# The down-projection of a gated MLP as seven products of half blocks in place of eight, with the sums of its left operands made in the up-projection's loop

## The chip, the cores and the metric

The kernel runs on one core of a Trainium2 chip. The metric is the device time of one execution in microseconds (us); the time quoted is the median of the runs shown. The engines are TensorE (PE, with its loads of the stationary operand as PEld), VectorE (DVE), ScalarE (ACT), GpSimd (POOL) and SyncE (SP), which in this kernel issues all DMA transfers.

## The reference

One encoder layer is applied to two sequences of 512 tokens with 1024 features, with shared weights. Only its last part, the gated MLP, is touched:

```python
h2 = _rmsnorm(x, g_ffn) * (1 + sc2) + sh2
u = _dwconv(h2 @ w_up, conv_w, conv_b)        # width 3, along the tokens
ua, ug = jnp.split(u, 2, axis=-1)             # 2816 features each
x = x + gt2 * ((jax.nn.silu(ug) * ua) @ w_down)
```

All arrays are float32, and the result is compared with a float32 reference, so a product of two matrices is made of three matmuls.

## The kernel before

**Split operands.** Each operand of a matmul is split into a high part (the value rounded to TensorE's fp32r format) and a low part (the rest). `mm3` (L78) multiplies high x high, high x low and low x high into one bank of PSUM. A split is a cast and a subtraction: `split_fast` (L74) makes the cast on ScalarE and the subtraction on VectorE, `split_pool` (L68) both on GpSimd.

**Order.** The code is written in program order, with tiles taken from pools of a fixed number of buffers. A scheduler that knows the dependencies and has a cost for each instruction puts the instructions of each engine into an order when the kernel is built; on the chip each engine, and SyncE's queue, goes through its list in that order.

**Up-projection** (L893 to L1007). It runs over 22 feature blocks `c` of 128 value and 128 gate features. Per block both sequences are made at once, as seven products of half blocks (12 matmuls each, `product`, L929) into three banks `px`, `py`, `pz`. The weights' sums for them are made on GpSimd (L913 to L919), the casts of the seven weight tiles on ScalarE, their subtractions on VectorE (four) and GpSimd (three) (`split_w`, L897). The products are copied and added into two value and two gate blocks; `conv1` (L941) makes the convolution in scratch tiles `tmp_u` of two buffers each; `gated` (L951) applies the gate, multiplies in place in the scratch tile and stores the product to the DRAM tensor `g_d`. Blocks 0 to 3 are started early, beside the last preparation of the activations.

**Down-projection** (L1009 to L1053). The two sequences follow each other. For a sequence all eight banks are taken, one for each of four token tiles and two halves of the 1024 output features. A loop over the 22 blocks of the contraction loads the activation block from `g_d` and the two halves of a weight block, splits them (activation and first half with `split_fast`, second half with `split_pool`) into a slot `wd` of four kinds (`pt`, `h`, `st`, `h`), and multiplies 24 matmuls. The last three blocks (`LATE`, L1014) are multiplied bank by bank, so that a bank is read out while the next ones are still multiplied. Reading out is a multiplication by the gate `gt` (L1051), an addition of the residual `xe` (L1052) and a store (L1053).

Raw weights and activations pass through six `wraw` tiles (L718), split weights of the up-projection through eight `wt` tiles (L723). The large tiles `h` (four buffers), `st` and `pt` (two each) hold the activations' halves of the up-projection: `st` holds `e` and then `t4`, `pt` holds `h1` and `h2`, `h` holds `e2`, `t3`, `t2` and `t1`.

## Time and profile before

| what | value |
|---|---|
| time, median of 3 runs (1461.2 to 1464.67) | 1461.97 us |
| span of the profiled execution, which was taken apart from these runs | 1468.5 us |
| down-projection, first to last matmul in that execution | 1222.97 to 1463.68 us |
| TensorE, VectorE, ScalarE, GpSimd busy | 96%, 68%, 46%, 41% |
| mean granted clock of TensorE, share of full speed | 0.985 |

Times in the rows below are from the span's start. Busy time of TensorE counts overlapping matmuls once, while the mean duration of one matmul contains the overlap with its neighbours. A row with `[x <- y]` says how long the engine stood idle before, and what ended that.

### The profile page before, as it was taken

What the parts mean: (1) busy time and instruction counts of PE and PEld (TensorE: products, weight loads), DVE (VectorE), ACT (ScalarE), POOL (GpSimd) and SP (SyncE); (2) the same over time, 40 slices, a digit from 0 to 9 for tenths busy, and PEclk for the clock granted to TensorE, in tenths of its full rate; (3) what the DMA queues carried; (4) which work ended last, traced back from release to release, by engine and by line L of the source; (5) the groups of instructions that cost most, each with busy time, mean ns of one, the idle gap of its engine ahead of it and who ended that gap; (6) DMA issues with size and microseconds to landing.
All of it is one profiled execution on the core that took longest, in us unless ns stands there. A gap on an engine that the chain in (4) does not pass through costs nothing.

```text
span 1468.5 us, 20794 instructions
## 1 busy us (share of the span) xinstructions
PE 1403.9 (96%) x7184; PEld 1161.6 (79%) x7184; DVE 1002.9 (68%) x1903; ACT 675.9 (46%) x1381; POOL 596.5 (41%) x600
## 2 busy tenths in 40 slices
PE   5889997999999999999998999999999999999998
PEld 4677876888888888878887777888888887888887
DVE  4788875666678886544479988777777777446433
ACT  3375222666666665422246455555555554122210
POOL 3365123442433442381004755555555535444430
PEclk9899999999999999999998999999999999999999
DMA  8456773222222213756302322222222227546522
GB/s 320 155 193 203 239 255 133 90 97 94 94 72 87 94 53 124 247 176 207 121 38 73 122 72 87 86 80 86 87 87 81 85 88 247 198 139 226 184 87 72
DMA packets 107801, 193.82 MB, mean 132 GB/s; under 512 B 18856, under 2 KB 39592, under 8 KB 104624
## 3 DMA queue, kind: packets, MB, share of 16 engines
q1 hardware_dynamic: 107696, 192.49, 39.6%
q8 instruction: 57, 0.93, 0.3%
q14 instruction: 48, 0.39, 0.1%
HBM read 148.39 MB, written 44.06 MB: 131 GB/s over the span
## 4 chain that ended last, share of the span: by engine, by line
PE 76%; DVE 15%; ACT 3%; POOL 2%; issue 2%; DMA 2%; SPq 0%; ACTq 0%; DVEq 0%; POOLq 0%
PE px L933 13%; PE psg L484 10%; PE py L933 6%; PE psd L81 5%; PE psd L79 5%; PE psd L80 5%; PE pz L933 3%; PE ppt L505 3%; PE ppo L568 2%; PE psz L79 2%; PE psx L81 2%; PE psx L80 2%; PE psx L79 2%; PE psz L81 2%; PE psy L81 2%
## 5 line engine op out<-in xcount | busy, mean ns | idle before, releaser
L933 PE MATMUL px<-t,wt 128*128 128x512 f32 x792 | 194.2, 395 | 7.6 <-ACT tmp_cc L938 6.6
L900 POOL TENSOR_TENSOR wt<-wraw,wt 128x512 fp32r<-128x512 f32 x66 | 91.5, 1390 | 238.3 <-ACT wt L899 238.2
L933 PEld LDWEIGHTS px<-t,wt 128*128 128x128 f32 x792 | 150.3, 191 | 42.1 <-ACT tmp_cc L938 9.4
L484 PE MATMUL psg<-h_hi,wg 128*128 128x512 f32 x512 | 169.8, 397 | 0.0
L499 POOL TENSOR_SCALAR p<-p,l 128x512 f32<-128x512 f32 (+2 forms) x128 | 78.2, 613 | 203.5 <-DVE l L498 128.8
L76 DVE TENSOR_TENSOR wd<-wraw,wd 128x512 fp32r<-128x512 f32 x88 | 95.5, 1124 | 94.5 <-ACT wd L75 94.4
L79 PE MATMUL psd<-wd 128*128 128x512 f32 x352 | 137.1, 389 | 1.3 <-DVE tmp_u L947 1.3
L81 PE MATMUL psd<-wd 128*128 128x512 f32 x352 | 137.0, 389 | 0.0
L80 PE MATMUL psd<-wd 128*128 128x512 f32 x352 | 136.9, 389 | 0.0
L75 ACT CAST wd<-wraw 128x512 fp32r<-128x512 f32 x88 | 50.9, 619 | 156.9 <-issue 108.4
L484 PEld LDWEIGHTS psg<-h_hi,wg 128*128 128x128 f32 x512 | 95.7, 189 | 18.4 <-POOL wg L72 0.8
L484 PE MATMUL psg<-h_lo,wg 128*128 128x512 f32 x256 | 101.6, 397 | 0.0
L497 ACT ACTIVATE p<-pps,nm 128x512 f32<-128x512 f32 (+2 forms) x128 | 78.1, 610 | 39.8 <-DVE nm L494 32.1
L945 DVE SCALAR_TENSOR_TENSOR tmp_u<-tmp_cc,cw,tmp_u 128x511 f32<-128x511 f32 x66 | 65.5, 993 | 39.4 <-ACT tmp_u L944 39.4
L900 DVE TENSOR_TENSOR wt<-tmp_sf,wt 128x512 fp32r<-128x512 f32 x88 | 82.2, 943 | 11.8 <-ACT wt L899 11.4
L79 PEld LDWEIGHTS psd<-wd 128*128 128x128 f32 x352 | 66.1, 188 | 15.5 <-issue 1.7
L69 POOL TENSOR_SCALAR wd<-wraw 128x512 fp32r<-128x512 f32 x44 | 30.6, 695 | 116.1 <-PE psd L81 77.9
L80 PEld LDWEIGHTS psd<-wd 128*128 128x128 f32 x352 | 66.1, 188 | 13.8
L494 DVE TENSOR_REDUCE nm<-pps 128x1 f32<-128x512 f32 (+2 forms) x128 | 74.7, 583 | 3.1 <-PE pps L81 1.5
L81 PEld LDWEIGHTS psd<-wd 128*128 128x128 f32 x352 | 66.1, 188 | 13.6
L72 POOL TENSOR_TENSOR wd<-wraw,wd 128x512 fp32r<-128x512 f32 x44 | 73.2, 1663 | 3.7
L947 DVE SCALAR_TENSOR_TENSOR tmp_u<-tmp_cc,cw,tmp_u 128x511 f32<-128x511 f32 x66 | 72.9, 1105 | 1.4
(257 smaller groups left out, 3516.0 us busy)
## 6 DMA issues: line engine op xcount, KB each, us to landing
w_ada<-in_w_ada_dram SPq DMA_DIRECT2D x24, 1024.0 KB, 6.3
wraw<-in_w_up_dram SPq DMA_DIRECT2D x96, 256.0 KB, 2.7
wraw<-in_w_down_dram SPq DMA_DIRECT2D x88, 256.0 KB, 3.5
g_d<-tmp_u SPq DMA_DIRECT2D x44, 256.0 KB, 2.3
wraw<-g_d SPq DMA_DIRECT2D x44, 256.0 KB, 3.4
wg_raw<-in_w_g_dram SPq DMA_DIRECT2D x16, 512.0 KB, 3.8
gate_d<-go SPq DMA_DIRECT2D x32, 256.0 KB, 2.0
ldb<-qb_d SPq DMA_DIRECT2D x8, 1024.0 KB, 5.0
```

The costliest lines, as they stand in the source:

```text
L72: G.tensor_sub(lo, raw, hi.bitcast(F32))
L76: V.tensor_sub(lo, raw, hi.bitcast(F32))
L79: PE.matmul(ps, lhsT=lh, rhs=rh, start=first, stop=False)
L80: PE.matmul(ps, lhsT=lh, rhs=rl, start=False, stop=False)
L81: PE.matmul(ps, lhsT=ll, rhs=rh, start=False, stop=last)
L484: PE.matmul(ps, lhsT=w[:, wl, m, k, :], rhs=hl[b][:, k, :], start=k == 0 and n == 0, stop=k == KD - 1 and n == 2)
L494: V.tensor_reduce(nm, ps[:, :n], op=ALU.max, axis=AX.X, negate=True)
L497: A.activation(p[:, :n], ps[:, :n], AF.Exp, bias=nm, accum_out=l)
L499: G.tensor_scalar(out=p[:, :plen], in0=p[:, :plen], scalar1=l, scalar2=1.0, op0=ALU.mult, op1=ALU.mult)
L900: lo_eng.tensor_sub(w[:, 1], raw, w[:, 0].bitcast(F32))
L933: PE.matmul(ps[:, sl], lhsT=w[:, wl, i], rhs=h[:, hl, sl], start=not add and i == 0 and n == 0, stop=i == 3 and n == 2, skip_group_check=add)
L947: V.scalar_tensor_tensor(out=u[:, 0:S - 1], in0=src[:, 1:S], scalar=cw[:, cc, 2:3], in1=u[:, 0:S - 1], op0=ALU.mult, op1=ALU.add)
```

## The change

The product of the activations A (rows: sequence 1, sequence 2; columns: blocks 0 to 10, blocks 11 to 21) and the weights B (the same halves of the contraction by two halves of the output features) is made as seven products of half blocks. Their left operands are A11, A12, A22, S1 = A21 + A22, S2 = S1 - A11, S3 = A11 - A21 and S4 = A12 - S2; their right operands are B11, B21, B22, and sums of blocks of B, kept in tiles `T`. Each product has 11 steps of 12 matmuls into a set of four banks; there are two sets.

In the up-projection the blocks go in the order 0, 11, 1, 12, and so on. `gated` writes the product into a tile `gs` of eight slots, and A11, A12 and A22 are stored from there. After each pair, `left_sums` makes S1 to S4 with four GpSimd operations and stores them: seven stores for a pair in place of four. `gs` has an `st` tile, and so have the two tiles `tq` of the down-projection, which hold `T[0..7]`, and `T[8..10]` with the first product `q1`.

In the down-projection each step loads one left operand and splits it with `split_fast`, four steps to a tile `gl`; the weight is split with `split_fast` into a `wt` tile. The sums of weights (in b11, b22, t2, t3) are made on GpSimd. The sets of banks are read out as the seven `product` calls at the end say; A12, S4, S3 and A22 accumulate on what their set holds already. Only the last product multiplies its last three steps bank by bank.

```diff
-    g_d = dram.tile([NB, NP, 128, S], F32, name="g_d")
+    a_d = dram.tile([7, HP, 128, S], F32, name="a_d")          # HP = 11
...
         def gated(c, b, ua, ug):
             A.activation(ug, ug, AF.Silu)
-            V.tensor_mul(ua, ua, ug)
-            SY.dma_start(g_d[b, c], ua)
+            k, j = divmod(c, HP)
+            g = gs[:, (6 * j + 2 * k + b) % 8]
+            V.tensor_mul(g, ua, ug)
+            if not (b and not k):
+                SY.dma_start(a_d[LEFT[f"A{b + 1}{k + 1}"], j], g)
+
+        def left_sums(j):
+            a11, a21, a12, a22, s1, s2 = (gs[:, (6 * j + i) % 8] for i in range(6))
+            G.tensor_add(s1, a21, a22)
+            SY.dma_start(a_d[LEFT["S1"], j], s1)
+            G.tensor_sub(a21, a11, a21)
+            SY.dma_start(a_d[LEFT["S3"], j], a21)
+            G.tensor_sub(s2, s1, a11)
+            SY.dma_start(a_d[LEFT["S2"], j], s2)
+            G.tensor_sub(a12, a12, s2)
+            SY.dma_start(a_d[LEFT["S4"], j], a12)
...
+        order = [j + k * HP for j in range(HP) for k in range(2)]
+        gs = mblk("gs", "st", [128, 8, S], F32)
+        for n, c in enumerate(order):
             ...
+            if c >= HP:
+                left_sums(c - HP)
...
-    (the whole down-projection, L1009 to L1053)
+        gts = []                                                # the gates of both sequences
+        sets = [[bank("psd") for _ in range(NT)] for _ in range(2)]
+        def left(name, j):
+            n = next(turn)
+            if n % 4 == 0:
+                tag = ("pt", "h", "pt", "h", "h")[n // 4 % 5]
+                blocks["g"] = hblk("gl", [128, 4, 2, S]) if tag == "h" else mblk("gl", tag, [128, 4, 2, S])
+            g = blocks["g"][:, n % 4]
+            split_fast(g[:, 0], g[:, 1], wraw(a_d[LEFT[name], j]))
+            return g
+        def right(raw):
+            w = wtile()
+            split_fast(w[:, 0], w[:, 1], raw)
+            return w
+        def tile_product(ps, i, w, g, first, last, add):
+            sl = slice(i * 128, (i + 1) * 128)
+            for n, (gi, wi) in enumerate(((0, 0), (0, 1), (1, 0))):
+                PE.matmul(ps, lhsT=g[:, gi, sl], rhs=w[:, wi], start=first and not add and n == 0,
+                          stop=last and n == 2, skip_group_check=add)
+        def product(which, name, weight, add, done, late=0):
+            pss, steps = sets[which], []
+            for j in range(HP):
+                steps.append((weight(j), left(name, j)))
+                if j < HP - late:
+                    for i in range(NT):
+                        tile_product(pss[i], i, *steps[j], j == 0, j == HP - 1, add)
+            for i in range(NT):
+                for j in range(HP - late, HP):
+                    tile_product(pss[i], i, *steps[j], j == 0, j == HP - 1, add)
+                done(i, pss[i])
+        tq = [mblk(f"tq{m}", "st", [128, 8, S], F32) for m in range(2)]
+        T = [tq[j // 8][:, j % 8] for j in range(HP)]
+        q1 = [tq[1][:, 4 + i] for i in range(NT)]
+        vw = hblk("vw", [128, 2, NT, S], F32)
+        def b11(j):
+            SY.dma_start(T[j], wd(0, 1, j))
+            raw = wraw(wd(0, 0, j))
+            w = right(raw)
+            G.tensor_sub(T[j], T[j], raw)
+            return w
+        def b21(j):
+            return right(wraw(wd(1, 0, j)))
+        def t1(j):
+            return right(T[j])
+        def b22(j):
+            raw = wraw(wd(1, 1, j))
+            w = right(raw)
+            G.tensor_sub(T[j], raw, T[j])
+            return w
+        def t2(j):
+            w = right(T[j])
+            G.tensor_sub(T[j], wraw(wd(1, 0, j)), T[j])
+            return w
+        def t3(j):
+            raw = wraw(wd(1, 1, j))
+            G.tensor_sub(raw, raw, wraw(wd(0, 1, j)))
+            return right(raw)
+        def c11(i, ps):
+            xt, y = x1_tile(0, i, 0), ytile()
+            V.tensor_mul(y, ps, gcols(0, 0))
+            V.tensor_add(y, y, xt)
+            store(0, i, 0, y)
+        def with_rest(b, m):
+            def done(i, ps):
+                xt, y = x1_tile(b, i, 1), ytile()
+                V.tensor_add(y, ps, vw[:, m, i])
+                G.tensor_mul(y, y, gcols(b, 1))
+                G.tensor_add(y, y, xt)
+                store(b, i, 1, y)
+            return done
+        def p5(i, ps):
+            V.tensor_add(vw[:, 0, i], ps, q1[i])
+        def p3(i, ps):
+            V.tensor_add(vw[:, 1, i], ps, q1[i])
+            xt = x1_tile(1, i, 0)
+            G.tensor_mul(q1[i], q1[i], gcols(1, 0))
+            G.tensor_add(q1[i], q1[i], xt)
+        def c21(i, ps):
+            y = ytile()
+            V.tensor_mul(y, ps, gcols(1, 0))
+            V.tensor_add(y, y, q1[i])
+            store(1, i, 0, y)
+        product(0, "A11", b11, False, lambda i, ps: A.copy(q1[i], ps))
+        product(0, "A12", b21, True, c11)
+        product(1, "S1", t1, False, p5)
+        product(1, "S4", b22, True, p3)
+        product(0, "S2", t2, False, with_rest(0, 1))
+        product(0, "S3", t3, True, with_rest(1, 0))
+        product(0, "A22", t1, True, c21, LATE)
```

## Rows read from the trace of the kernel before

**Rows 1.** The page's first part: busy time, share of the span, instructions.
```profile
span 1468.5 us, 20794 instructions
...
PE 1403.9 (96%) x7184; PEld 1161.6 (79%) x7184; DVE 1002.9 (68%) x1903; ACT 675.9 (46%) x1381; POOL 596.5 (41%) x600
```

**Rows 2.** Busy time by stretch; the columns stand in the first line.
```profile
core 0: us, PE busy (x) PEld busy (x) DVE busy (x) ACT busy (x) POOL busy (x), PEclk, DMA share, GB/s
800.00:840.00 40.00, 36.96 (x155) 29.73 (x154) 39.09 (x38) 22.94 (x40) 29.60 (x18) 0.96 0.28 88
840.00:887.00 47.00, 42.61 (x181) 33.11 (x179) 39.33 (x48) 25.00 (x42) 25.85 (x16) 1.00 0.30 94
1000.00:1019.04 19.04, 19.04 (x85) 15.77 (x85) 13.37 (x16) 9.57 (x17) 9.91 (x8) 1.00 0.25 83
1019.04:1038.08 19.04, 19.04 (x85) 15.77 (x85) 15.75 (x19) 11.22 (x19) 9.58 (x8) 1.00 0.27 83
...
1222.97:1251.00 28.03, 26.76 (x118) 21.86 (x117) 19.17 (x21) 9.67 (x16) 14.24 (x13) 1.00 0.78 252
1346.50:1464.10 117.60, 117.56 (x519) 97.06 (x517) 47.02 (x49) 17.34 (x30) 38.14 (x32) 1.00 0.39 130
```

**Rows 3.** The chain of waits in order of time: start, us, engine or DMA, tile.
```profile
838.76 3.52 DMA g_d<-tmp_u
...
883.79 2.02 DMA g_d<-tmp_u
...
1194.91 2.72 PE py L933 x12
```

**Rows 4.** Groups of the down-projection, 1190 us to the end: busy us, mean ns | idle before.
```profile
L79 PE MATMUL psd<-wd 128*128 128x512 f32 x352 | 137.1, 389 | 1.3 <-DVE tmp_u L947 1.3
...
L76 DVE TENSOR_TENSOR wd<-wraw,wd 128x512 fp32r<-128x512 f32 x88 | 95.5, 1124 | 94.5 <-ACT wd L75 94.4
L72 POOL TENSOR_TENSOR wd<-wraw,wd 128x512 fp32r<-128x512 f32 x44 | 73.2, 1663 | 3.7
...
L75 ACT CAST wd<-wraw 128x512 fp32r<-128x512 f32 x88 | 50.9, 619 | 156.9 <-issue 108.4 <-PE psd L81 26.3 <-DMA wraw<-g_d 16.8
```

**Rows 5.** Timeline of VectorE and GpSimd, single subtractions: start, us, engine.
```profile
800.47 0.68 DVE L76 TENSOR_TENSOR t<-e,t 128x512 fp32r<-128x512 f32 x1
801.07 0.68 DVE L76 TENSOR_TENSOR t<-tmp_sf,t 128x512 fp32r<-128x512 f32 x1
...
1241.52 1.30 POOL L72 TENSOR_TENSOR wd<-wraw,wd 128x512 fp32r<-128x512 f32 x1
...
1247.20 2.39 DVE L76 TENSOR_TENSOR wd<-wraw,wd 128x512 fp32r<-128x512 f32 x2 [2.82 <-ACT wd L75]
1247.27 1.77 POOL L72 TENSOR_TENSOR wd<-wraw,wd 128x512 fp32r<-128x512 f32 x1
...
1323.97 1.78 DVE L76 TENSOR_TENSOR wd<-wraw,wd 128x512 fp32r<-128x512 f32 x1
```

**Rows 6.** DMA issues: KB each, median us from issue to landing.
```profile
wraw<-in_w_down_dram SPq DMA_DIRECT2D x88, 256.0 KB, 3.5
...
wraw<-g_d SPq DMA_DIRECT2D x44, 256.0 KB, 3.4
```

**Rows 7.** Timeline of the handover into the down-projection, and of its end.
```profile
1217.37 0.62 ACT L75 CAST wd<-wraw 128x512 fp32r<-128x512 f32 x1 [2.88 <-DMA wraw<-g_d]
...
1218.52 4.61 PE L933 MATMUL px<-t,wt 128*128 128x512 f32 x12 [1.86 <-ACT tmp_cc L938]
...
1229.18 0.47 PE L79 MATMUL psd<-wd 128*128 128x512 f32 x1 [1.27 <-DVE tmp_u L947]
...
1463.68 0.39 PE L81 MATMUL psd<-wd 128*128 128x512 f32 x1
1464.10 0.69 DVE L1051 TENSOR_TENSOR ye<-psd,gtf 128x512 f32<-128x512 f32 x1 [0.62 <-PE psd L81]
```

More of the change, by code (lines that the diff above doesn't have):

```diff
@@ L34 @@
 NP = FF // 128
+HP = NP // 2
+LEFT = {n: i for i, n in enumerate(("A11", "A12", "A22", "S1", "S2", "S3", "S4"))}
 EPS = 1e-6
@@ L986, in encoder_block @@
         EARLY, HALVES = 4, 2
-        wf = [list(weights_first(c)) for c in range(HALVES)]
+        order = [j + k * HP for j in range(HP) for k in range(2)]
+        wf = [list(weights_first(c)) for c in order[:HALVES]]
         banks = [(bank("px"), bank("pz")) for _ in wf]
@@ L997, in encoder_block @@
         differences(0, 2)
-        for c in range(HALVES, EARLY):
-            started.append(first(weights_first(c)))
-            differences(c, c + 1)
-        for c in range(NP):
-            if c < EARLY:
-                rest(c, weights_rest(c), *started[c])
+        for n in range(HALVES, EARLY):
+            started.append(first(weights_first(order[n])))
+            differences(n, n + 1)
+        gs = mblk("gs", "st", [128, 8, S], F32)
+        for n, c in enumerate(order):
+            if n < EARLY:
+                rest(c, weights_rest(c), *started[n])
             else:
@@ new lines, in encoder_block @@
+            gts.append(gt)
+        sets = [[bank("psd") for _ in range(NT)] for _ in range(2)]
+        turn = iter(range(7 * HP))
+        blocks = {}
+        def left(name, j):
[6 more added lines that the diff above has]
+            return g
@@ new lines, in wd @@
+        def wd(k, n, j):
+            return w_down[(k * HP + j) * 128:(k * HP + j + 1) * 128, n * 512:(n + 1) * 512]
+        def right(raw):
[7 more added lines that the diff above has]
+                          stop=last and n == 2, skip_group_check=add)
@@ L1046, in encoder_block @@
-                SY.dma_start(xt, x1_d[t * 128:(t + 1) * 128, :])
-                for hf in range(2):
-                    products(i, NP - LATE, NP, (hf,))
-                    cs = slice(hf * 512, (hf + 1) * 512)
-                    y = wk.tile([128, 512], F32, name="ye", bufs=2)
-                    V.tensor_mul(y, pss[i][hf], gt[:, cs])
-                    V.tensor_add(xt[:, cs], xt[:, cs], y)
-                    SY.dma_start(out[t * 128:(t + 1) * 128, cs], xt[:, cs])
+                for j in range(HP - late, HP):
+                    tile_product(pss[i], i, *steps[j], j == 0, j == HP - 1, add)
@@ new lines, in product, with x1_tile, store @@
+                done(i, pss[i])
[3 more added lines that the diff above has]
+        vw = hblk("vw", [128, 2, NT, S], F32)
+        def x1_tile(b, i, n):
+            xt = wk.tile([128, 512], F32, name="xe", bufs=6)
+            t = b * NT + i
+            SY.dma_start(xt, x1_d[t * 128:(t + 1) * 128, n * 512:(n + 1) * 512])
+            return xt
+        def store(b, i, n, src):
+            t = b * NT + i
+            SY.dma_start(out[t * 128:(t + 1) * 128, n * 512:(n + 1) * 512], src)
@@ new lines, in ytile, with gcols @@
+        def ytile():
+            return wk.tile([128, 512], F32, name="ye", bufs=4)
+        def gcols(b, n):
+            return gts[b][:, n * 512:(n + 1) * 512]
+        def b11(j):
[13 more added lines that the diff above has]
+            return w
```

30 lines of the change are left out of this document (2 added, 28 removed).

## The prediction, made before the changed kernel was run

> **What bounds the kernel now.** I read the page's first part, then the stretches, the chain of waits, the groups of the down-projection, and last the timeline of the two engines that prepare its operands. TensorE is busy for 96% of the span, VectorE for 68%, GpSimd for 41% [rows 1]. By stretch [rows 2]: from 1000 to 1038 us (up-projection) TensorE never pauses, VectorE works 13.37 to 15.75 us and GpSimd 9.6 to 9.9 us of each 19.04 us, which is one feature block's seven products. From 1346.50 to 1464.10 us (down-projection) TensorE is full again, VectorE at 47 of 118 us. The chain of waits is TensorE alone there: twelve matmuls take 2.72 us [rows 3], so one costs 0.2267 us, not the 389 ns that the groups print, since matmuls overlap [rows 4]. The exception is 800 to 887 us: VectorE is busy 39.09 of 40 us, TensorE loses matmuls, and the chain passes through four stores of the gated product (first 3.52, last 2.02 us), because the scratch tile that was stored must be free before the next convolution [rows 2, 3]. So the change works where TensorE sets the time; the question is what it costs the engines that feed TensorE.
>
> **Matmuls.** The code gives 2 sequences x 22 blocks x 4 token tiles x 2 halves x 3 = 1056 now (three lines of 352 [rows 4]) and 7 products x 11 x 4 x 3 = 924 after. 132 fewer x 0.2267 = **-29.9 us**. Stationary loads stay one per matmul.
>
> **Preparation in the down-projection.** A step is now 12 matmuls, 2.72 us, and needs two splits (activation, weight): 154 ScalarE casts and 154 VectorE subtractions, against 88 and 88 now [rows 4]. ScalarE: 2 x 0.62 = 1.24 us of 2.72, hidden. VectorE: a subtraction alone takes 0.68 us and the next starts after 0.60; beside a GpSimd operation it takes 1.78 [rows 5]. GpSimd's two-input operation alone takes 1.30 us [rows 5]. The weight sums (11 each in b11, b22, t2, t3) give 44 of these; p3 adds 8, with_rest 16: 68 in all, for the 44 tensor_tensor and 44 tensor_scalar of now.
>
> What two subtractions and one GpSimd operation cost together is a row: VectorE's pair lasts 2.39 us with GpSimd's 1.77 us inside [rows 5]. That is below 2.72, so such a step is still TensorE's, by 0.33 us; a step without a GpSimd sum needs about 1.2. The Trainium skill (SBUF — State Buffer, "Who interferes with whom") says that a VectorE instruction with two SBUF inputs and a GpSimd instruction that reads SBUF exclude each other, the later one blocking until the first is done. The trace agrees nearly (2.39 measured, 0.60 + 0.60 + 1.30 = 2.50 by strict exclusion); by the rule the next sum would be some 3.6 us larger.
>
> The tight stretch is S4, S2, S3: 33 steps x 2.39 = 79 us, and p3 and the first with_rest put 16 x 1.30 = 21 us of GpSimd work in between: 100 us for 33 x 2.72 = 90 us of matmuls. Ahead of it stands S1, whose steps are cheap: the eight split-weight tiles let preparation run some six steps, 14 us, ahead, which just covers the 10 us. In S3 a step also needs three raw tiles. One lives for its load, 3.5 us [rows 6], then 1.3 to 1.8 for the sum, 0.6 for the cast, 0.7 to 1.8 for the subtraction: by these about 8 us for one and 5.5 for each of the others, 19 over six tiles, 3.2 us a step, 0.5 x 11 = 5 us over. Bounds 0 (the lead covers all) to +15 (it covers nothing); I take **+3 us**, since the lead is nearly as long as what it has to cover.
>
> **Product boundaries.** Four times a product accumulates into the set of banks just read out (A12, S4, S3, A22). A bank is free again for the nine matmuls of the other three, 2.04 us; an eviction starts 0.03 us after its last matmul ends and takes 0.69 [rows 7]. It fits if VectorE stands ready. One contended subtraction ahead (1.78) makes it 0.5 us late, and what is queued behind the waiting eviction on VectorE are the next product's subtractions. Bounds 0 to 3 us each; I take 1, nearer to the fitting case: **+4 us**. S1 and S2 enter the other set and wait for nothing. The last product keeps the late three steps, so the end after the last matmul (1463.68 to 1468.5 us [rows 1, 7]) stays.
>
> **Handover.** Now ScalarE's cast waits 2.88 us for an activation load ahead of a copy that TensorE needs; TensorE waits 1.86 us, then runs its next twelve at a lower rate (4.61 instead of 2.88 us), and waits 1.27 us for a bank later [rows 7]: 4.9 us. Afterwards only four banks must be free, and the raw tiles of b11, held until T is loaded, limit how far ahead loads crowd in. Against that T may be loaded only once the last t4 product is done, and T[8..10] only after the last sums are stored. About five steps (13.6 us) lie ready; T's load (3.5), its subtraction (1.3) and the next raw load and split (3.5 + 1.3) take 9.6. Three loads a step, 786 KB in 2.72 us, are 289 GB/s, against 252 at a share of 0.78 now [rows 2], so 0.89. Bounds -4.9 to +5; I take **0**, both having causes of the same size.
>
> **Up-projection.** Four GpSimd operations per two blocks: 44. Each may hold a VectorE operation for 1.78 - 0.68 = 1.10 us, so up to 4.4 us per 38 us. VectorE's gaps are 5.7 and 3.3 us in the two blocks shown [rows 2], 9.0 a pair; GpSimd grows from 19.5 to about 25 of 38 us. The cover is there on average. SyncE's stores grow from four to seven a pair; the loads queued behind them for the next block have a block's time. Bounds 0 to +12 (each pair over by 1.1, one added operation); I take **+2**. In the early stretch VectorE has no gap until 840 us and 7.7 us until 887 [rows 2]; two groups of sums, 8 x 1.10 = 8.8 us, come there. On the other hand the product now goes to a tile of its own, and the waits for the stores leave the chain. TensorE ran 181 matmuls where 207 fit, so at most 5.9 us is to be had. Bounds -5.9 to +8.8, taken at **+1**: VectorE is scarcest there, and the gain needs ScalarE alone.
>
> **Sum.** -29.9 + 3 + 4 + 0 + 2 + 1 = -19.9. The profiled execution spans 1468.5 us, 6.5 more than the median 1461.97 of the runs timed without it; I let that difference stand: span 1448.6, **predicted time 1442 us**.
>
> **Rivals.** (a) *Everything hides*: the lead covers the sums, the boundaries fit and the early stretch gains: -30 to -36, 1426 to 1432 us. For it: 2.39 under 2.72 and full TensorE with all these operations now. Against: 100 us of preparation for 90 of matmuls. (b) *Preparation bounds the down-projection*: the 44 steps with a GpSimd sum go at the 3.2 us of the raw tiles, +21 instead of +3: 1460 us with the other terms as they are, about 1457 if the boundaries then hide in it. For it: six raw tiles, each waiting in turn for load, GpSimd, ScalarE and VectorE. Against: only S3 needs three, and b21 and t1 leave room. (c) *The sums slow the up-projection*, the one that ends slower. VectorE and GpSimd take their work in a fixed order, so gaps that lie elsewhere don't help; if each of the 44 sums cost its full 1.10 us, that is 48 us, and with the rest of the sum (-22.9) the time is 1487. It decides from 0.68 us per sum on (29.9 / 44), 0.52 with my other terms. For it: 800 to 840 us, where 38 VectorE and 18 GpSimd operations filled 40 us [rows 2], or 18 and 8.6 per 19 us, and the block would then need 17 and 9. Against: in the steady stretch weights are split well ahead and TensorE shows no pause.
>
> **Chances.** Forecast (1433 to 1453) 0.57; (a) 0.13; (b) 0.16; (c) in part or whole 0.14, of which half ends slower. Range: leaving out (c)'s slower half and the best of (a), 1430 to 1460; the forecast's own is 1433 to 1453. Below 0.3%, 4.4 us, no difference can be told. Faster: 0.13 + 0.57 + half of (b) + some of (c) = 0.80. Same: 0.10. Slower: 0.10.
>
> **What would show it.** Right: 924 matmuls at 0.2267 us; about 210 us of them between the last up-projection product and the end; VectorE near 2.4 us a step in S4 to S3; pauses of a microsecond at four boundaries. Wrong: TensorE pauses inside S2 or S3 waiting for a split (b), or a block of the up-projection longer than 19.04 us in the steady stretch (c); pauses over 2 us that bring the lower rate would add to either.

## The result: slower by 0.95%

| | before | after |
|---|---|---|
| time, median of 4 runs each | 1463.32 us (1461.2 to 1464.7) | 1476.86 us (1474.35 to 1482.6) |
| ratio, 95% interval | | 1.0095 [1.0072, 1.0118] |

The forecast was 1442 us. The change cost 13.5 us where 19.9 were to be gained. (In the runs below, one of the eight executions of e2_order took 2281.22 us; it is in that run's median and in no ratio.) The page of the changed kernel has 132 matmuls less [rows 1], as counted:

```profile
span 1474.8 us, 20829 instructions
...
PE 1373.5 (93%) x7052; PEld 1133.5 (77%) x7052; DVE 1092.2 (74%) x1969; ACT 711.7 (48%) x1451; POOL 681.2 (46%) x624
```

TensorE is busy 30.4 us less, in a span 6.3 us longer. Where its pauses are, the timeline of the down-projection's matmuls tells (start, us, engine; a run of matmuls without a pause is one row):

```profile
1217.91 13.76 PE L1068 MATMUL psd<-wt,gl 128*128 128x512 f32 x60
1242.45 139.18 PE L1068 MATMUL psd<-wt,gl 128*128 128x512 f32 x600 [10.78 <-ACT gl L77]
1400.41 32.65 PE L1068 MATMUL psd<-wt,gl 128*128 128x512 f32 x132 [18.77 <-DVE ye L1143]
1437.33 32.94 PE L1068 MATMUL psd<-wt,gl 128*128 128x512 f32 x132 [4.27 <-DVE ye L1143]
```

Five steps (60 matmuls) are ready when the up-projection ends; then TensorE waits 10.78 us for an activation. A11, A12, S1, S4 and S2 follow without a pause, so two of the four boundaries (A12, S4) cost nothing. Ahead of S3 and ahead of A22 it waits 18.77 and 4.27 us for a read-out: 33.8 us of pauses, where before there was one of 1.27 [rows 4, 7].

The same, by stretch (columns as in [rows 2]): a pair of feature blocks of the up-projection; the handover; the 20 us behind it; the surroundings of the long pause.

```profile
938.89:977.78 38.89, 38.39 (x170) 31.47 (x169) 36.77 (x35) 20.26 (x35) 28.97 (x19) 1.00 0.31 104
1220.00:1240.00 20.00, 11.67 (x52) 9.34 (x50) 4.99 (x5) 1.27 (x2) 13.82 (x10) 0.88 0.56 199
1242.45:1262.45 20.00, 20.00 (x75) 16.27 (x76) 14.07 (x15) 10.48 (x18) 7.77 (x5) 0.84 0.80 282
1262.45:1380.00 117.55, 117.55 (x520) 97.37 (x519) 77.33 (x103) 50.74 (x88) 45.84 (x32) 1.00 0.63 210
1345.00:1400.00 55.00, 36.63 (x162) 30.02 (x160) 26.88 (x33) 15.94 (x28) 33.10 (x24) 0.87 0.59 193
```

Two blocks now take 38.89 us, not 38.08 [rows 2]: VectorE is busy 36.77 of them (29.1 before) and GpSimd 28.97 (19.5). And the pauses have an echo: in the 20 us behind the handover the granted clock is 0.84, a mean between the two levels, and TensorE makes 75 matmuls where 88 would fit.

**Where the 13.8 us between the two profiles are** (both counted from the up-projection's first matmul; what lies ahead of it varies from run to run, 767.9 to 775.8 us over all profiles here, with identical code):

| part | before | after | difference |
|---|---|---|---|
| first matmul to the pair from which the blocks run steadily (by its product `pz`) | 141.92 | 142.48 | +0.6 |
| 15 steady blocks | 285.6 | 291.2 | +5.6 |
| from there to the first down-projection matmul | 20.07 | 16.32 | -3.75 |
| down-projection to the end | 245.53 | 256.89 | +11.4 |

Of the 11.4 us in the last line 11.0 are found: -29.9 of matmuls, +32.5 of pauses (33.8 less the 1.27 of before), and 8.4 us by which the last three runs of matmuls outlast their count at 0.2267 us (3.0, 2.6 and 2.9), behind the pauses.

**The long pause.** VectorE's timeline around it (start, us):

```profile
1374.50 1.78 DVE L78 TENSOR_TENSOR wt<-tq,wt 128x512 fp32r<-128x512 f32 x1
1379.04 0.69 DVE L78 TENSOR_TENSOR gl<-wraw,gl 128x512 fp32r<-128x512 f32 x1 [2.75 <-ACT gl L77]
...
1395.53 0.69 DVE L78 TENSOR_TENSOR gl<-wraw,gl 128x512 fp32r<-128x512 f32 x1 [1.78 <-ACT gl L77]
1396.14 0.68 DVE L78 TENSOR_TENSOR wt<-wraw,wt 128x512 fp32r<-128x512 f32 x1
1398.97 0.69 DVE L78 TENSOR_TENSOR gl<-wraw,gl 128x512 fp32r<-128x512 f32 x1 [2.15 <-ACT gl L77]
1399.58 2.48 DVE L1143 TENSOR_TENSOR ye<-psd,vw 128x512 f32<-128x512 f32 x4
```

S2's last subtraction is at 1374.50, its last matmul ends at 1381.6. The read-out of S2 (L1143) would need 0.69 us then, and S3 waits for it, because S3 accumulates into S2's banks. But in VectorE's list six and a half steps of S3 come first, and they come one per 3.32 us (1379.04 to 1398.97, six intervals), because each waits for a cast, and the cast for a load: VectorE is idle more than half of that time, with a ready read-out in its list behind work that isn't ready.

Why the steps are late shows on GpSimd, in SyncE's queue and in ScalarE's wait for S2's last step (start, us):

```profile
1363.29 3.43 POOL L1156 TENSOR_TENSOR tq<-tq,xe 128x512 f32<-128x512 f32 x2
...
1380.82 1.28 POOL L1131 TENSOR_TENSOR wraw<-wraw 128x512 f32<-128x512 f32 x1 [1.92 <-issue]
```
```profile
1365.05 2.02 SPq L1092 DMA_DIRECT2D xe<-x_d  x2
1367.17 2.40 SPq L722 DMA_DIRECT2D wraw<-in_w_down_dram  x2
1369.67 0.38 SPq L722 DMA_DIRECT2D wraw<-a_d  x1
...
1379.76 0.93 SPq L722 DMA_DIRECT2D wraw<-in_w_down_dram  x2
1382.12 0.33 SPq L722 DMA_DIRECT2D wraw<-a_d  x1
```
```profile
1373.24 0.62 ACT L77 CAST gl<-wraw 128x512 fp32r<-128x512 f32 x1 [12.13 <-DMA wraw<-a_d]
```

The loads of the residual `xe` for S2's read-out wait 8.8 us for the additions of `p3` on GpSimd (L1156), which use the tiles that these loads fill. The next operand's load stands behind them in the queue, and ScalarE's cast waits 12.13 us for it. In S3 the loads then wait for raw tiles: those at 1379.76 and 1382.12 us are issued 0.03 and 0.02 us after VectorE's subtraction (from 1379.04) and GpSimd's sum of weights (L1131) have freed one.

**The handover.** SyncE's queue (start, us):

```profile
1218.10 2.70 SPq L1106 DMA_DIRECT2D tq<-in_w_down_dram  x6
1223.49 2.02 SPq L959 DMA_DIRECT2D a_d<-gs  x2
...
1234.99 0.32 SPq L971 DMA_DIRECT2D a_d<-gs  x1
1235.40 0.87 SPq L1042 DMA_DIRECT2D gtf<-gt_d  x2
1236.32 0.42 SPq L722 DMA_DIRECT2D wraw<-a_d  x1
```

The load on which TensorE waits is issued at 1236.32, behind six stores of the last pair, the last of which waits for the last sum on GpSimd.

**The pair.** VectorE and GpSimd take turns, in a stretch with the sums (L964 to L970):

```profile
959.10 3.48 DVE L902 TENSOR_TENSOR wt<-tmp_sf,wt 128x512 fp32r<-128x512 f32 x2
962.50 1.79 DVE L997 TENSOR_TENSOR tmp_cc<-tmp_cc 128x512 f32<-128x512 f32 x1
964.21 1.78 DVE L902 TENSOR_TENSOR wt<-tmp_sf,wt 128x512 fp32r<-128x512 f32 x1
965.91 0.68 DVE L998 TENSOR_TENSOR tmp_cc<-tmp_cc,py 128x512 f32<-128x512 f32 x1
```
```profile
958.59 1.73 POOL L966 TENSOR_TENSOR gs<-gs 128x512 f32<-128x512 f32 x1
960.28 1.74 POOL L968 TENSOR_TENSOR gs<-gs 128x512 f32<-128x512 f32 x1
961.98 1.76 POOL L916 TENSOR_TENSOR tmp_sf<-tmp_sf,wraw 128x512 f32<-128x512 f32 x1
963.69 1.75 POOL L970 TENSOR_TENSOR gs<-gs 128x512 f32<-128x512 f32 x1
965.40 1.76 POOL L919 TENSOR_TENSOR tmp_sf<-wraw 128x512 f32<-128x512 f32 x1
```

Each engine starts an operation every 1.70 us, in step with the other. The one VectorE operation that reads a PSUM bank (L998, `py`) takes 0.68 beside a GpSimd one. The Trainium skill (SBUF — State Buffer, "Who interferes with whom") states that a VectorE instruction with at most one SBUF input, outside the modes that use both ports, doesn't contend with GpSimd; the trace agrees.

### The profile page after: what moved, and what is told of

Read it like the earlier page. It is cut to its first block, busy times and chain, and to the rows that moved or that the text cites. A ratio compares the mean times of both kernels' runs of the same rounds, so it can differ in the third digit from the quotient of the medians.

```text
span 1474.8 us, 20829 instructions
## 1 busy us (share of the span) xinstructions
PE 1373.5 (93%) x7052; PEld 1133.5 (77%) x7052; DVE 1092.2 (74%) x1969; ACT 711.7 (48%) x1451; POOL 681.2 (46%) x624
## 4 chain that ended last, share of the span: by engine, by line
PE 59%; DVE 22%; POOL 6%; issue 5%; ACT 5%; DMA 4%; SPq 0%; POOLq 0%; DVEq 0%; ACTq 0%
PE psg L486 10%; PE px L935 8%; PE psd L1068 7%; PE py L935 4%; DVE tmp_u L947 3%; DVE wt L902 3%; PE ppt L507 3%; DVE tmp_u L949 2%; PE pz L935 2%; PE ppo L570 2%; PE psz L81 2%; DMA wraw<-a_d 2%; PE psz L83 2%; PE psx L83 2%; PE psx L82 2%
## 5 line engine op out<-in xcount | busy, mean ns | idle before, releaser
L1068 PE MATMUL psd<-wt,gl 128*128 128x512 f32 x924 | 218.5, 400 | 33.8 <-DVE ye L1143 23.0
L1068 PEld LDWEIGHTS psd<-wt,gl 128*128 128x128 f32 x924 | 179.1, 194 | 73.1 <-ACT wt L77 19.2
L78 DVE TENSOR_TENSOR gl<-wraw,gl 128x512 fp32r<-128x512 f32 x77 | 60.4, 799 | 62.8 <-ACT gl L77 62.8
L77 ACT CAST gl<-wraw 128x512 fp32r<-128x512 f32 x77 | 46.9, 620 | 85.1 <-DMA wraw<-a_d 84.7
L946 ACT ACTIVATE tmp_u<-tmp_cc,cw 128x512 f32<-128x512 f32 x66 | 53.6, 812 | 62.2 <-DVE tmp_cc L998 56.2
L935 PE MATMUL px<-h,wt 128*128 128x512 f32 (+1 forms) x288 | 67.7, 380 | 2.8 <-POOL wt L902 2.4
L81 PE MATMUL psz<-wz,h_hi 128*128 128x384 f32 (+1 forms) x176 | 63.6, 361 | 5.9 <-DVE h_hi L115 3.5
L935 PE MATMUL py<-e,wt 128*128 128x512 f32 x264 | 63.8, 391 | 5.2 <-ACT tmp_cc L940 5.2
L935 PE MATMUL pz<-h,wt 128*128 128x512 f32 (+1 forms) x288 | 66.3, 375 | 0.0
L507 PE MATMUL ppt<-ident,p 128*128 128x128 f32 x416 | 66.2, 272 | 0.0
```

What stands on the lines that cost most here:

```text
L78: V.tensor_sub(lo, raw, hi.bitcast(F32))
L81: PE.matmul(ps, lhsT=lh, rhs=rh, start=first, stop=False)
L507: PE.transpose(pt[:, j * 128:(j + 1) * 128], p[:, j * 128:(j + 1) * 128], ident)
L935: PE.matmul(ps[:, sl], lhsT=w[:, wl, i], rhs=h[:, hl, sl], start=not add and i == 0 and n == 0, stop=i == 3 and n == 2, skip_group_check=add)
L1068: PE.matmul(ps, lhsT=g[:, gi, sl], rhs=w[:, wi], start=first and not add and n == 0, stop=last and n == 2, skip_group_check=add)
```

## The experiments

Sixteen kernels ran, each compared with the kernel before on the same chip. They ran on several chips, so runs are compared by their ratios (the kernel before took 1463.3 to 1467.2 us on them). The pauses are those of one profiled execution, which can stand some microseconds from the median (e6_three: 1463.01 us for 1459.68; e12_sums_queue: 1456.17 for 1462.32). The pauses are TensorE's in the down-projection, from its first matmul on (in the two runs with raw tiles for activations alone, from the up-projection's last): at the handover and in A11, and around S3 and A22.

| run | ratio to before, 95% | median us | handover, A11 | S3, A22 |
|---|---|---|---|---|
| the change | 1.0095 [1.0072, 1.0118] | 1476.86 | 10.8 | 23.0 |
| e1_no_sums | 0.9971 [0.9953, 0.9989] | 1462.59 | 3.6 | 24.0 |
| e2_order | 1.0042 [1.0022, 1.0062] | 1474.55 | 11.2 | 12.7 |
| e3_queue | 1.0061 [1.0041, 1.0081] | 1476.38 | 5.9 | 24.8 |
| e4_both | 1.0008 [0.9991, 1.0024] | 1468.22 | 6.2 | 13.8 |
| e5_readout | 1.0033 [1.0015, 1.0050] | 1471.12 | 10.8 | 13.3 |
| e6_three | 0.9951 [0.9935, 0.9968] | 1459.68 | 6.0 | 7.5 |
| e7_raw | 1.0005 [0.9989, 1.0021] | 1466.59 | 5.4 | 4.6 |
| e8_three_no_sums | 0.9858 [0.9831, 0.9885] | 1444.76 | 2.7 | 7.6 |
| e9_spread | 0.9946 [0.9927, 0.9964] | 1458.78 | 6.1 | 6.9 |
| e10_own_raw | 1.0094 [1.0070, 1.0118] | 1479.91 | 21.3 | 7.7 |
| e11_spread_raw | 1.0093 [1.0071, 1.0115] | 1478.44 | 23.4 | 5.4 |
| e12_sums_queue | 0.9969 [0.9954, 0.9985] | 1462.32 | 5.3 | 5.2 |
| e13_s3_raw | 0.9893 [0.9871, 0.9914] | 1450.93 | 5.5 | 1.9 |
| e14_all | 0.9907 [0.9886, 0.9928] | 1453.00 | 5.1 | 1.8 |
| e15_raw_alone | 1.0086 [1.0061, 1.0112] | 1478.05 | 10.8 | 20.0 |
| e16_raw_order | 0.9989 [0.9973, 1.0006] | 1464.94 | 11.0 | 8.4 |

### The sums (e1_no_sums)

```diff
-            G.tensor_add(s1, a21, a22)
-            SY.dma_start(a_d[LEFT["S1"], j], s1)
+            SY.dma_start(a_d[LEFT["S1"], j], a22)
```

and so for the other three, whose slots get a21, a12 and a11.

> Leaves out the four GpSimd sums of each pair of blocks in the up-projection (the places of S1 to S4 receive unsummed products, so the output is not the reference's); the 77 stores and all of the down-projection stay. Theory A (GpSimd's sums hold VectorE up, so a pair of blocks takes 38.89 us in place of 38.08): the pairs between 900 and 1175 us return to 38.08 us, the up-projection becomes some 6 us shorter. Rival (the seven stores, or the new order of the blocks, make the pair longer): 38.89 us stays. The last pair's stores then wait for no sum either, so SyncE's queue is free sooner at the handover: TensorE's wait of 10.8 us there should shrink to under 4 if these stores are its cause. The waits of 18.8 and 4.3 us in the down-projection are untouched by it in theory B (VectorE's order of work): they stay within 3 us. Time: about 1477 - 6 - 9 = 1462 us.

The steady pairs go back to 38.08 us with VectorE at 30.68, although the seven stores remain:

```profile
913.09:951.17 38.08, 38.08 (x170) 31.53 (x169) 30.68 (x35) 20.91 (x34) 19.87 (x15) 1.00 0.31 104
```

So the lengthening of the pairs is the four sums', and not the stores'. The handover's pause falls to 3.56 us, as it would if the stores held the queue because they waited for sums; GpSimd has less to do there as well, and e3_queue moves the stores alone. The pauses at S3 and A22 stay. By the ratios the sums cost 0.0124, about 18 us in all. In the two profiles, from the up-projection's first matmul on, they are 5.6 us in the steady pairs, 2.3 in the early stretch, and at the handover 7.2 of pause and 2.5 of lower rate behind it.

### Order, queue and read-outs (e2 to e6)

The order: from the fourth step of S3 and of A22 on, VectorE's subtractions are put behind the read-out that the product waits for (`issue_after` sets the order within one engine's list).

```diff
+                with tc.issue_after(behind) if behind is not None and j >= 3 else ExitStack():
                     steps.append((weight(j), left(name, j)))
...
-        product(0, "S2", t2, False, with_rest(0, 1))
-        product(0, "S3", t3, True, with_rest(1, 0))
-        product(0, "A22", t1, True, c21, LATE)
+        read = product(0, "S2", t2, False, with_rest(0, 1))
+        read = product(0, "S3", t3, True, with_rest(1, 0), behind=read)
+        product(0, "A22", t1, True, c21, LATE, behind=read)
```

> The same work; only VectorE's order in the down-projection is changed: the subtractions of S3's and A22's steps from the fourth on stand behind the reading out of the product before. Theory B (the 18.8 and 4.3 us are a matter of order: the reading out stands behind eight late steps of the next product): both waits fall to under 3 us each, the time by 15 to 20 us, to 1457 to 1462. Rival C (preparation is too slow in S2 and S3 anyway; the order only decides where TensorE waits): the two waits vanish from the boundaries, but TensorE waits inside S3 for casts, 15 us or more in sum, and the time stays within 6 us of 1477. The handover's 10.8 us and the pair's 38.89 us stay in both.

The 18.8 us became 5.7, but 5.2 us came up inside S3, where the next steps are still late. The order is a cause; it isn't the whole of it. The pauses are 10.4 us shorter and the ratio 0.0053 lower, some 8 us: between theory B's 15 to 20 and rival C's 6 at most.

The queue: the last pair's six stores are issued by ScalarE.

```diff
-                SY.dma_start(a_d[LEFT[f"A{b + 1}{k + 1}"], j], g)
+                (A if c == NP - 1 else SY).dma_start(a_d[LEFT[f"A{b + 1}{k + 1}"], j], g)
...
+            Q = A if j == HP - 1 else SY
...
-            SY.dma_start(a_d[LEFT["S1"], j], s1)
+            Q.dma_start(a_d[LEFT["S1"], j], s1)
```

> The same work; only the six stores of the last pair of blocks are issued from ScalarE's queue in place of SyncE's. Theory D (at the handover the loads of the sixth step and on stand in SyncE's queue behind the stores of the last pair, which wait for VectorE and GpSimd): SyncE issues these loads about 10 us sooner, TensorE's wait of 10.8 us falls under 4, the time by 7 to 12 us, to 1465 to 1470. Rival E (the raw tiles of b11, held until T is loaded, are what is late): the loads move by less than 3 us and the wait stays above 8. The waits of 18.8 and 4.3 us stay.

The handover's pause falls from 10.8 to 4.4 us (5.9 with two short ones), but the ratio only from 1.0095 to 1.0061, with intervals that overlap: the pause at S3 grew by 1.7. Theory D's 7 to 12 us did not come.

The fourth kernel has both edits.

> The edits of e2_order and e3_queue together. If theories B and D hold and are independent: 1477 - 17 - 9 = 1451 us, under the kernel before (1463) by some 12 us. If rival C holds: about 1468. If C and E hold: about 1477.

1468.22 us is the time that rival C gave, and 5.8 us of pauses stand inside S3. The two together bring the kernel level with the one before, no further. SyncE's queue shows what still holds S3 up:

```profile
1398.99 0.34 SPq L1100 DMA_DIRECT2D out_dram<-ye  x1
1399.39 0.42 SPq L1095 DMA_DIRECT2D xe<-x_d  x1
1403.70 4.19 SPq L1100 DMA_DIRECT2D out_dram<-ye  x3
1407.98 0.87 SPq L722 DMA_DIRECT2D wraw<-in_w_down_dram  x2
```

For nine microseconds no weight is loaded: the output stores wait for GpSimd's multiplication and addition of the read-out (eight operations in a row), and S3's loads stand behind the stores. Hence the next edit, with `with_rest` and `p3` on VectorE:

```diff
-                G.tensor_mul(y, y, gcols(b, 1))
-                G.tensor_add(y, y, xt)
+                V.tensor_mul(y, y, gcols(b, 1))
+                V.tensor_add(y, y, xt)
```

> The changed kernel with one edit: the gate multiplication and the residual addition of the read-outs with_rest and p3 on VectorE instead of GpSimd (24 GpSimd operations fewer). Theory D (GpSimd's bursts in the read-outs hold back the weight sums, and the stores and loads queued behind them on SyncE): the pause between S2 and S3 (18.8 us) falls by 8 to 14 us and the one before A22 (4.3) goes or stays under 2; the time is 1461 to 1469. Theory B (VectorE's fixed order alone: the read-out stands behind eight steps of the next product, whatever makes those late): the pause stays at 15 or more, since the two added VectorE operations per read-out stand in the same order; 1473 to 1480. The waits at the handover (10.8) and the up-projection stay by either.

By itself it took 6.3 us off the long pause (12.5 left) and nearly all of the one ahead of A22: between the two theories, so both have a part.

The sixth has all three edits.

> The three edits together: the subtractions of S3 and A22 from the fourth step on behind the read-out, the last pair's six stores from ScalarE's queue, and the read-outs on VectorE alone. If the waits add up as separate ones (order: 23 to 13; queue: 10.8 to 6; read-outs: most of the remaining 13 between S2 and the end), TensorE's idle time in the down-projection is about 10 us, against 20 with the first two, and the time 1456 to 1461: below the kernel before. Rival: what is left after the first two is the three raw tiles that a step of S3 needs, and not the bursts; then the time stays at 1466 to 1470.

The three together give 1459.68 us, as forecast from separate waits, and beat the kernel before, though the pauses sum to 13.5 us and not to 10. In the ratio the three edits gave 0.0053, 0.0034 and 0.0062 alone and 0.0144 together, so they add up. The pause that is left inside S3 is 5.45 us:

```profile
1408.22 1.22 PE L1069 MATMUL psd<-wt,gl 128*128 128x512 f32 x2 [5.45 <-ACT gl L77]
```

### The raw tiles (e7, e10, e13, e15, e16)

On top of the three edits, one tile more in the pool that all stages share:

```diff
-        r = wp.tile([128, 512], F32, name="wraw", bufs=6)
+        r = wp.tile([128, 512], F32, name="wraw", bufs=7)
```

> The three edits together, and seven raw tiles for six. My estimate for S3 was 19 us of raw-tile life per step over six tiles, 3.2 us a step, against 2.72 of matmuls; with seven it is 2.7. If raw tiles set S3's pace, its pauses shrink by up to 5 us against the run with six, and loads at the handover come earlier as well, so 3 to 6 us off the time. If they do not, the two times agree within 1.5 us.

The down-projection went from 236.1 to 230.2 us, the pause inside S3 from 5.45 to 0.82, but the steady pairs went to 39.6 to 39.8 us, and the time is 6.9 us longer than e6_three's: with a seventh tile GpSimd's splits and sums in the up-projection stand in another order. The shared pool mixes two effects.

The next takes the down-projection's activation loads out of that pool instead:

```diff
-            split_fast(g[:, 0], g[:, 1], wraw(a_d[LEFT[name], j]))
+            raw = wk.tile([128, 512], F32, name="lraw", bufs=2)
+            SY.dma_start(raw, a_d[LEFT[name], j])
+            split_fast(g[:, 0], g[:, 1], raw)
```

> The three edits together, and two more raw tiles that only the down-projection's activation loads use, in that stage's own pool (with seven tiles shared by all stages the down-projection took 230.3 us for 236.1, but the up-projection's steady pairs 39.7 us for 38.9). If raw tiles set S3's pace and nothing in the up-projection hangs on them, the pairs stay at 38.88 us, the down-projection goes to 229 to 232 us, and the time is 1453 to 1456. Rival: the loads ahead crowd the up-projection's last blocks through SyncE's queue, or the seventh tile's gain was only the shift of the instructions' order; then 1458 or more.

The rival's 1458 or more came, but by neither of its ways: the run is 20 us slower than e6_three, at the handover.

```profile
1242.05 32.32 PE L1071 MATMUL psd<-wt,gl 128*128 128x512 f32 x132 [17.80 <-ACT gl L77]
```

Nothing was ready when the up-projection ended. The first two loads into the stage's own tiles were issued at 1232.62 us, after the up-projection. The five ready steps of the change come from loads into the shared raw tiles, made while the up-projection still runs. I read the late issue as memory that the old stage still holds: the loads of `gtf`, also tiles of the new stage and just ahead in the queue, wait 3.2 us for VectorE's last multiplication in `gated` (L957). No run tests this reading. Part of the 17.80 us is another wait: ScalarE's first cast of these tiles is at 1241.38 us, behind the last pair's stores in its own queue, of which the last is issued at 1240.96.

S3's second weight tile can be given its own place without touching the handover:

```diff
             raw = wraw(wd(1, 1, j))
-            G.tensor_sub(raw, raw, wraw(wd(0, 1, j)))
+            other = wk.tile([128, 512], F32, name="r3", bufs=2)
+            SY.dma_start(other, wd(0, 1, j))
+            G.tensor_sub(raw, raw, other)
```

> The three edits together, and in S3 the second weight tile of a step is loaded into one of two tiles of the stage's own, so that a step takes two of the six raw tiles instead of three; up-projection and handover are untouched. By the raw-tile estimate (19 us of tile life per step over six tiles, 3.2 us; two tiles fewer in demand give about 13.5 over six, 2.25 us) the 5.45 us pause inside S3 falls below 1 us, the down-projection goes from 236 to 229 to 232 us, and the time is 1453 to 1456. Rival: with seven shared tiles that pause went for another reason (the order of the engines shifted); then it stays at 4 us or more and the time at 1458 to 1461.

1450.93 us: 16.2 us under the kernel before on the same chip, and the best that ran. Timeline of the matmuls:

```profile
1223.38 13.76 PE L1069 MATMUL psd<-wt,gl 128*128 128x512 f32 x60
1241.51 19.93 PE L1069 MATMUL psd<-wt,gl 128*128 128x512 f32 x75 [4.36 <-ACT gl L77]
1262.55 122.15 PE L1069 MATMUL psd<-wt,gl 128*128 128x512 f32 x537 [1.12 <-ACT tq L1170]
1386.45 30.23 PE L1069 MATMUL psd<-wt,gl 128*128 128x512 f32 x132 [1.75 <-DVE ye L1148]
1416.84 27.53 PE L1069 MATMUL psd<-wt,gl 128*128 128x512 f32 x120 [0.17 <-DVE ye L1148]
```

The down-projection takes 225.5 us (span 1448.9 less 1223.38), and from S3 on the echo is gone with the pauses: the last two rows are 132 and 120 matmuls at 0.228 us. Behind the handover's 4.36 us it is still there: the 75 matmuls take 2.8 us more than their count. The gain on e6_three is 0.0058 of the time, 8.5 us, more than the 5.45 us pause: over the whole stage the pauses are 6.1 us shorter, and the lower rate behind them costs nearly 4 us less.

Then this edit alone on the change, and with the order of e2_order.

> The changed kernel with the one edit of S3's own two raw tiles, and none of the other three. If the raw tiles are the root of the pause before S3 (18.8 us) and the fixed order and GpSimd's bursts only pass it on, that pause falls below 6 us, the one before A22 (4.3) below 2, and the time is 1456 to 1462 on 1476.9. If the order is the root (the read-out behind eight steps that bursts and queue make late in any case), 10 us or more of the pause stays and the time is 1466 to 1474.

The tiles alone bring nothing that the ratio tells from the change: the long pause is still there.

```profile
1406.38 32.88 PE L1068 MATMUL psd<-wt,gl 128*128 128x512 f32 x132 [18.04 <-DVE ye L1145]
```

S3's steps came one per 3.02 us here (VectorE's subtractions from 1386.19 to 1404.30 us, six intervals), not at the estimated 2.25. The two new tiles now hold the loads up: one is loaded again at 1398.05 us, 0.04 us after GpSimd's sum has freed it. Seven steps stood ahead of the read-out in place of six and a half. So this run doesn't tell what the pause would be with fast steps and the old order.

> The changed kernel with S3's own two raw tiles and with the subtractions of S3 and A22 behind the read-out; the last pair's stores and GpSimd's share of the read-outs as in the change. The order alone gave 1474.6, with 12.7 us of pauses from S3 on. If tiles and order together are what S3 needs, those pauses fall below 4 us and the handover's 11 us stays: 1458 to 1463. If GpSimd's bursts are needed too, 6 us or more of pauses stay: 1465 to 1470.

Tiles and order leave 8.4 us of pauses, as the second theory had it; tiles, order and read-outs (e13_s3_raw, with the queue's edit, which acts at the handover) leave 1.9. From the 23.0 us at S3 and A22 the order alone took 10.4, the read-outs alone 9.8, the tiles alone 3.1. So the long pause has two parts: a read-out that stands behind S3's steps, and steps that are late, by GpSimd's bursts and by the raw tiles. In the ratio the tiles are worth 0.0009 alone, 0.0053 on top of the order and 0.0058 on top of the three edits.

### Handover and pairs again (e8, e9, e11, e12, e14)

First the sums' price in the mended kernel, by the edit of e1_no_sums on top of the three.

> The three edits together, and the four GpSimd sums per pair of feature blocks left out (the four slots then hold the unsummed blocks, so the output is not the reference's). What is left is the seven products with their preparation and read-outs. If the sums cost what they did in the unrepaired kernel (0.81 us per steady pair, some 8 us and a few at the handover), it is 8 to 14 us below the run of the three edits: 1444 to 1452, near the forecast of 1442. Rival: with the waits mended, the sums' part is hidden and the difference is under 4 us.

1444.76: the sums cost 14.9 us in the kernel of the three edits, somewhat more than expected. The two profiles are further apart, 18.1 us: 5.6 in the steady pairs, 6.3 in the early stretch (138.62 us without sums, 144.89 with them, 141.92 before), 4.4 in the down-projection and 1.8 ahead of the up-projection. The early stretch is the least sure of these, since it took 142.4 to 144.9 us in the profiles of the kernels with sums and six raw tiles; without sums it took 140.15 in e1_no_sums.

Then the sums spread over two blocks:

```diff
-            G.tensor_sub(s2, s1, a11)
+            if j == HP - 1:
+                late_sums(j)
...
+        def late_sums(j):
+            G.tensor_sub(s2, s1, a11)
...
             if c >= HP:
                 left_sums(c - HP)
+            elif c:
+                late_sums(c - 1)
```

> The three edits together, and the four sums of a pair spread over two blocks: S1 and S3 behind the pair's second block as before, S2 and S4 behind the first block of the next pair (the last pair's stay together). In the run of the three edits every second block takes 19.84 us and the others 19.04, so the lengthening stands where four sums come in a row. Theory A1 (clumping: GpSimd's four sums in one block hold VectorE up, while the other block has room): both blocks go at 19.04 to 19.2, some 6 to 9 us are gained, and the time is 1450 to 1454 on a run of the three edits at 1459.7. Rival A2 (any sum costs what it holds VectorE up, wherever it stands): the pair keeps 38.88 us, both blocks at 19.4; 1458 to 1461.

Every second block still took 19.8 to 19.9 us, but this doesn't decide between the two: GpSimd's timeline has all four sums together all the same.

```profile
960.39 1.74 POOL L965 TENSOR_TENSOR gs<-gs 128x512 f32<-128x512 f32 x1
...
963.81 1.74 POOL L967 TENSOR_TENSOR gs<-gs 128x512 f32<-128x512 f32 x1
965.52 1.73 POOL L975 TENSOR_TENSOR gs<-gs 128x512 f32<-128x512 f32 x1
...
968.92 1.73 POOL L977 TENSOR_TENSOR gs<-gs 128x512 f32<-128x512 f32 x1
```

Where the code has them does not set where they run; the scheduler does. Whether spread sums would be hidden stays open.

With the spread sums and the two `lraw` tiles:

> All of it: the three edits, the sums spread over two blocks, and two raw tiles of the down-projection's own. If the two gains are separate, 1444 to 1449, near the run without any sums (1444.8). If one hides the other or the order of the engines shifts against it, above 1452.

The handover of the activations' own tiles again (17.47 us), and the sums aren't spread here either.

For the handover, the last sums' stores in the queue of the engine that makes the sums:

```diff
-            Q = A if j == HP - 1 else SY
+            Q = G if j == HP - 1 else SY
```

> The three edits together, but the last pair's four stores of sums on GpSimd's own queue instead of ScalarE's (the engine that makes the sums issues their stores, so nothing else stands behind the wait; the two stores of the gated product stay on ScalarE's). In the run of the three edits ScalarE stood 11.6 us behind these stores before it could cast the next activation block, and TensorE waited 4.15 us for that cast. If the wait is the queue's, TensorE's pause falls to 0 to 2 us, and 2 to 5 us are gained: 1455 to 1458. Rival: the cast's load, issued at 1229.28 and behind the loads of T, or GpSimd's own five operations ahead are what is late; then 1459 to 1461.

No gain: the 4.15 us became 1.30 and 2.37 us waits on the next step. ScalarE now waited 6.75 us for a weight's load instead of for its own stores, while GpSimd had T's subtractions, the sums and their stores to do one after the other from 1225.06 to 1245.13. The time is just above the rival's 1459 to 1461, and the trace is as it has it: at the handover, loads and GpSimd's work are what is late once the stores are out of the way.

The last combines this with S3's own tiles.

> Both of these at once. If the two waits are separate places, the gains add: 1450 to 1454, with under 6 us of TensorE's idle time left in the down-projection and the rest of the distance to 1442 in the up-projection's pairs (38.88 us for 38.08, some 6 us) and the lower clock behind a pause. If one wait only moves to the next, 1455 to 1459.

1453.00 us lies in the range given for gains that add, but e12_sums_queue had gained nothing to add: the time is not below that of e13_s3_raw.

## Why the prediction was wrong

The terms of its sum, and what the two profiles gave:

| term | predicted | measured |
|---|---|---|
| matmuls | -29.9 | -29.9: 924, and 60 of them in 13.76 us |
| up-projection, steady | +2 (0 to 12) | +5.6 |
| early stretch | +1 (-5.9 to +8.8) | +0.6 |
| handover | 0 (-4.9 to +5) | -3.75 ahead of the first matmul, +10.8 pause, about +3 of lower rate, -1.3 for the old wait: +8.8 |
| boundaries and preparation | +4 and +3 | +23.0 and about +5.5 of lower rate behind them |

- **The step that failed is "Product boundaries".** It said that "what is queued behind the waiting eviction on VectorE are the next product's subtractions", and gave each boundary 0 to 3 us. On the chip they are queued ahead of it. Two boundaries cost nothing, the other two 18.77 and 4.27 us. I counted the eight split-weight tiles as a lead that covers late work; by my reading the same eight tiles let the scheduler list six and a half steps of S3 ahead of S2's read-out, and when those are late, the read-out is as late as they are. e2_order shows the order's part, e5_readout that of the late steps, e15_raw_alone that without the order the tiles help next to nothing.
- **The rate of S3 was near, its price wrong.** "3.2 us a step" by the raw tiles: 3.32 was measured, and the loads do wait for freed tiles. The sum of tile lives behind it isn't confirmed: with two tiles less in demand it gave 2.25, and e15_raw_alone went at 3.02, held up by its two new tiles. I charged the excess over TensorE's 2.72, 0.5 us for eleven steps. But since the read-out stands behind those steps and TensorE stands still meanwhile, nothing of a step is covered: 18 us from S2's last matmul to the read-out. That is more than the +15 that I had set as the worst case of the preparation. Rival (b) had this rate too, but its sign, a pause inside S3 for a split, does not show in the change; it shows (5.20 us) once e2_order moves the read-out.
- **GpSimd's bursts** were in the sum as work (21 us between the steps), not as what stands in SyncE's queue: output stores and `xe` loads wait for them, and the next product's loads wait behind those. That was the part that e5_readout and e6_three took out.
- **Handover.** The five ready steps were right (60 matmuls in 13.76 us). The 9.6 us for T, its sum and the next load and split were too few: with the stores on another queue (e3_queue) the sixth step still starts 18.2 us after the first, without sums (e1_no_sums) 17.3. What I left out besides is that the six stores of the last pair stand between T's loads and the next activation's in one queue, and wait for VectorE and GpSimd. e3_queue shows it: the 10.8 us became 5.9.
- **The pairs.** Rival (c), the only one that ended slower, holds in a small part: 5.6 us for 28 sums in the seven steady pairs is 0.2 us each, far from the 0.68 that decides alone. The sums' whole cost, some 18 us by e1_no_sums, lies for more than half at the handover, which the rival didn't have. (Its "17 and 9" operations per block are 17.5 and 10 by [rows 2].) GpSimd's gain in busy time, 9.5 us a pair, was underestimated (25 of 38 us forecast, 28.97 of 38.89 measured), since a sum and the operations beside it take 1.73, not 1.30. The early stretch had both effects that the prediction named: without sums it is 1.8 and 3.3 us shorter than before (e1_no_sums, e8_three_no_sums), with them 0.5 to 3.0 longer.
- **The lower rate behind a pause** stood only in the last sentence, without a price. It cost 8.4 us, a quarter of what the pauses cost.

The difference of 6.5 us between span and median, which I let stand, did no harm: 13.8 us between the profiles, 13.5 in the timed runs.

What the change promised is there: with the read-outs mended, the last stores moved and two raw tiles more, the same seven products run 1.1% faster than before. In the profile of e13_s3_raw the up-projection costs 6.6 us (3 forecast), the handover 3.5 (0 forecast), and boundaries with preparation 2.2 in place of 7; so these -16.2 us come near the forecast's -19.9 partly because its errors cancel.

## What to carry to other kernels

Where a product must wait for a read-out of the banks that it accumulates into, look where that read-out stands in its engine's list: a deep lead of prepared operands can put the next product's late work in front of it, and the pause is the lateness of all that work, not the read-out's 0.7 us. Go through every queue that carries both loads and stores, and ask of each store which engine it waits for, since the loads behind it wait for the same. Mend order, queue, read-outs and buffers together before judging such a change: one at a time they gave 0.1 to 0.6%, all four 2.0%, and the edit that gave 0.1% alone gave 0.6% on top of the other three.

## What the runs showed of the hardware that was not expected

- Behind a pause of 10.8 us the granted clock was 0.84 over 20 us and 600 matmuls took 3.0 us more than their count; behind 18.8 and 4.3 us, 132 took 2.6 and 2.9 us more. Behind the last pauses of e13_s3_raw, 1.75 and 0.17 us, no such loss shows. That a pause is short doesn't settle it: in the kernel before, the twelve matmuls behind 1.86 us took 4.61 us for 2.88 [rows 7].
- VectorE and GpSimd in step at 1.70 us per operation each: the pair is done sooner than the two in turn (0.60 us from one start to the next on VectorE alone [rows 5], 1.25 on GpSimd alone at 1366.68 us of the changed kernel, 1.85 together).
- In the trace a ready read-out waits for 18 us behind subtractions that aren't ready, on an engine that is idle for more than half of that time. The Trainium skill (PSUM — Partial Sum Buffer, "Engine vs sequencer instructions") states that VectorE's queue is strictly first in, first out; the trace agrees.
